# The first layer's output product in one written order with alternating accumulators, and the last projection's partial sums loaded behind the next weights

## The chip, the cores and the metric

The kernel runs as one program on one core of a Trainium2 chip. Engines of that core work side by side, each through its own list of instructions in order: TensorE (PE, matrix products), VectorE (DVE), ScalarE (ACT), GpSimd (POOL) and SyncE (SP, which issues most transfers). An instruction waits on semaphores for what it needs. The metric is the device time of one execution in microseconds (us). The kernel before takes 1270.09 us, the median of three runs (1269.7 to 1270.78).

## What is computed

A stream x of 1024 tokens with 1024 channels goes through two layers; all data is fp32.

```python
# layer 0 (even): a convolution branch A and a recurrent branch B
va, vg, ga, xb, gb = split(h @ w_in)
y_a = conformer_conv(va, vg) * silu(ga)
y_b = rglru_branch(xb, h0 from the context) * silu(gb)
x = x + gate0 * (concatenate([y_a, y_b]) @ w_out)
# layer 1 (odd): pooling mixer
u, g = split(rmsnorm_and_modulate(x) @ w_in1)
y = grouped(pool(u) - u) * scale * silu(g)          # 2048 channels
x = x + gate1 * (y @ w_out1)
return rmsnorm(x, final_g)
```

## The kernel before

Channels lie on partitions and tokens along the free dimension, so x is eight tiles of 128x1024. A large product is computed as three products of rounded halves: `split` makes a high half by a cast on ACT (L98) and a low half by a subtraction on DVE (L99), and `prod` issues high by high (L1153), high by low data (L1155) and low by high (L1156), four times in turn, which makes twelve matmuls of 128x512.

The products of this case are done in two-by-two blocks with seven products in place of eight (a scheme like Strassen's). One call of `quad` makes two tiles of output channels, m and m+1, over both halves of the tokens. The seven operands of data are called b11, t1, t2, b21, t3, b22 and t4; the seven operands of weights, `wq_..._1` to `_7`, are made by `wquad_steps` from two raw loads of 512 KB (`wr_..._0` and `_1`, L1117) by sums on DVE (L1133 to L1142) and splits. There are two raw buffers, so the loads of the next block wait until the last reader of this block's raw weights has run. The products go into three accumulators of one PSUM bank each, a, b and c (tiles `qa`, `qb`, `qc`): b11 into a, which ACT copies to b; t1 into c; t2 on top of the copy in b; b21 on top of a; t3 on top of b; b22 on top of c; t4 on top of b. Between the products the content is read out: c after t1 goes to quarter (1,1), b after t2 to (0,1), a after b21 to (0,0), b after t3 to (1,1), c after b22 to (0,1), and b after t4 to (1,0). A product that adds to a bank has to wait until the reader of the bank's earlier content is done.

The first layer's output product of branch A is `woa`, four calls for m = 0, 2, 4, 6. Its `put` (L1470 to L1482) reads a partial stream back into an x tile, adds the gated accumulator with one DVE instruction (L1473), stores the tile, and adds its square to the sums of the next norm (L1459, L1462, L1463). After it on PE come folds of the second layer's weights, then eight blocks of that layer's products.

The second layer's output product comes in two parts over the input channels, `wo0` (m = 0 to 6) and `wo1`. `wo0` uses another function, `quad_linked`. There each product is made to follow the one before in the written order (`linked`), every second block takes other banks (`spare`: tiles `qac` and half of a wide tile), and the last product of a block (t4) is issued after the next block's b11 and t1 (`pend`). Its `put` loads a 256 KB piece xp of the stream kept in DRAM (L1908), adds the gated accumulator (`gated`, L1829) and stores the piece back from ACT's queue (`stores`, L1845).

The order of instructions on each engine is set when the kernel is built: a scheduler puts each instruction where its own model of time has it ready, `tc.high_priority` lets the read-outs of accumulators go ahead, and `tc.issue_after` keeps one instruction behind another. On the chip the order is fixed. In `woa` before, the order of the seven products on PE comes from that scheduler.

Of the kernel before, what the change touches and what calls it, by code (L numbers as in the profile page):

```python
# [20 lines left out]
KT = D // P  # L21
H = 512
HALF = (slice(0, H), slice(H, S))
# [28 lines left out]
def body(ctx, tc, xT, ctxT, cc, ccol, modT, modW, win, gw, wout, wu, grp, wg, wo1, small, edge, ident, outT):  # L52
# [1412 lines left out]
    def woa(m, w, ahead):  # L1465
# [17 lines left out]
        return quad(w, f"woa{m}", ya, put, ahead, m == KT - 2)  # L1483
# [45 lines left out]
    last["pe"] = ended_[0]  # L1529
# [310 lines left out]
    copied_, kept_out = [None], []  # L1840

    def stores(after, n):
        with held(after):
            for _ in range(n):
                nc.scalar.dma_start(*kept_out.pop(0))  # L1845

    chain = [None]

    def linked(*args):
        with held(chain[0]):  # L1850
            chain[0] = prod(*args)
        return chain[0]

    def spare(name):
        a, c = banks(f"qac_{name}", 0)
        return a, c, wide(f"qb_{name}")[:, HALF[1]]

    def quad_linked(w, name, ops, put, ahead, order, pend, other):
        p1, p2, p3, p4, p5, p6, p7 = w
        a, c, b = spare(name) if other else [psum(f"q{n}_{name}") for n in "acb"]  # L1860
        linked(a, p1, ops["b11"], True, False)
        with tc.high_priority(offset=EVAC):
            evac = nc.scalar.copy(b, a)
        linked(c, p5, ops["t1"], True, False)
        with tc.high_priority(offset=EVAC):
            put(1, 1, c, 0)
            stores(kept_[0], len(kept_out))
        if pend is not None:
            pend()
        linked(b, p6, ops["t2"], False, False)  # L1870
        with tc.high_priority(offset=EVAC):
            put(0, 1, b, 0)
        linked(a, p2, ops["b21"], False, True)
        with tc.high_priority(offset=EVAC):
            put(0, 0, a, None)
        with tc.issue_after(evac.ins):
            nxt_ = ahead()
        for name in order:
            if name == "t3":
                linked(b, p7, ops["t3"], False, False)  # L1880
                with tc.high_priority(offset=EVAC):
                    put(1, 1, b, 1)
            else:
                linked(c, p3, ops["b22"], False, True)
                with tc.high_priority(offset=EVAC):
                    put(0, 1, c, 1)
# [423 lines left out]
```

## Time and profile before

| quantity | value |
|---|---|
| median of three runs | 1270.09 us |
| the profiled execution's own time | 1268.66 us |
| its span from first to last instruction | 1266.9 us |
| PE busy | 1251.0 us, 99% |
| DVE busy | 1140.9 us, 90% |
| ACT busy | 655.1 us, 52% |
| POOL busy | 295.0 us, 23% |
| mean clock granted to TensorE | 0.996 |

Times in rows of the timeline are microseconds from the start of the span. A row gives the start, the busy time, the engine, the line, the operation, the output and inputs, how many were merged, and in brackets the idle time before it and who ended that. Issues of transfers stand under the queue of their engine (SPq, ACTq).

### The profile page before, as it was taken

To read this page: it belongs to the slowest core of one execution; us is meant where nothing else is said; L and a number is where in the kernel's file an instruction comes from. 1 tells how busy PE (TensorE), PEld (TensorE's weight loads), DVE (VectorE), ACT (ScalarE), POOL (GpSimd) and SP (SyncE) were. 2 spreads that over 40 slices of the span, in tenths; PEclk is the share of its full clock that TensorE was granted. 3 is DMA by queue.
4 is the path that set the end of the run, shared out by engine and by line. 5 is a ranking of instruction groups with operands and counts; after the bars stand their busy time and mean duration, and the time that the engine had idled before them with its cause. 6 is when DMAs were issued, how large, how long until landed. Compare 5 with 4: busy or idle time off the path is not lost. (4 is left out here: it accounts for less than half of the span.)

```text
span 1266.9 us, 16191 instructions
## 1 busy us (share of the span) xinstructions
PE 1251.0 (99%) x5858; PEld 1034.7 (82%) x5858; DVE 1140.9 (90%) x1748; ACT 655.1 (52%) x955; POOL 295.0 (23%) x176
## 2 busy tenths in 40 slices
PE   9999999999999999999999999999999999999996
PEld 7788888888888888888887888788888888877885
DVE  7799999999999999988978979999899987977976
ACT  8464566556666533237435446744343444634642
POOL 0015364436443547533210023000000000000003
PEclk9999999999999999999999999999999999999998
DMA  9971121112121234442437665243333334848723
GB/s 377 381 257 33 53 64 50 59 42 75 44 81 42 83 125 133 158 141 84 160 98 233 207 205 173 100 158 125 133 107 118 117 125 142 296 168 311 295 68 133
DMA packets 78705, 182.29 MB, mean 144 GB/s; under 512 B 7712, under 2 KB 23328, under 8 KB 78624
## 3 DMA queue, kind: packets, MB, share of 16 engines
q1 hardware_dynamic: 67328, 172.33, 39.8%
q10 hardware_dynamic: 11296, 8.92, 2.2%
q8 instruction: 46, 0.75, 0.2%
q14 instruction: 35, 0.29, 0.1%
HBM read 137.18 MB, written 44.04 MB: 143 GB/s over the span
## 5 line engine op out<-in xcount | busy, mean ns | idle before, releaser
L670 DVE SCALAR_TENSOR_TENSOR conv<-u,sm,conv 128x505 f32<-128x505 f32 (+6 forms) x224 | 153.8, 746 | 1.0
L2030 POOL TENSOR_TENSOR o<-x,rr 128x256 f32<-128x256 f32 (+1 forms) x10 | 9.7, 1008 | 449.5 <-ACT rr L2030 449.5
L670 ACT ACTIVATE l<-g,sm 128x512 f32<-128x512 f32 (+1 forms) x96 | 58.7, 619 | 57.7 <-PE g L670 57.0
L670 POOL TENSOR_TENSOR l<-l,l 128x1280 f32<-128x1280 f32 x16 | 47.1, 2966 | 25.6 <-ACT l L670 15.1
L98 ACT CAST wq_g<-wr_g 128x512 fp32r<-128x512 f32 x48 | 28.3, 621 | 43.4 <-DMA wr_g<-wg 16.1
L98 ACT CAST wq_wo<-wr_wo 128x512 fp32r<-128x512 f32 x48 | 28.6, 619 | 41.9 <-DMA wr_wo<-wo 20.9
L670 PE MATMUL va<-h0h,wl_va 128*128 128x512 f32 x128 | 49.9, 390 | 0.2 <-DVE wl_va L670 0.2
L670 PE MATMUL gb<-h0h,wl_gb 128*128 128x512 f32 x128 | 49.9, 390 | 0.2 <-POOL wl_gb L670 0.2
L670 PE MATMUL gb<-h0l,wh_gb 128*128 128x512 f32 x128 | 49.8, 389 | 0.0
L670 PE MATMUL gb<-h0h,wh_gb 128*128 128x512 f32 x128 | 49.8, 389 | 0.0
L670 PE MATMUL va<-h0l,wh_va 128*128 128x512 f32 x128 | 49.8, 389 | 0.0
L670 PE MATMUL va<-h0h,wh_va 128*128 128x512 f32 x128 | 49.8, 389 | 0.0
L670 PE MATMUL wob<-ybh,wh_wob 128*128 128x512 f32 x128 | 49.8, 389 | 0.0
L670 PE MATMUL wob<-ybl,wh_wob 128*128 128x512 f32 x128 | 49.8, 389 | 0.0
L670 PE MATMUL wob<-ybh,wl_wob 128*128 128x512 f32 x128 | 49.8, 389 | 0.0
L670 DVE TENSOR_TENSOR_SCAN l<-l,l 128x256 f32<-128x256 f32 (+1 forms) x32 | 48.7, 1521 | 1.1
L670 DVE SCALAR_TENSOR_TENSOR conv<-cL,wsum,conv 128x506 f32<-128x506 f32 (+3 forms) x70 | 48.2, 746 | 0.2
L670 POOL TENSOR_TENSOR l<-l,uc 128x1280 f32<-128x1280 f32 x16 | 47.7, 3008 | 0.0
L98 ACT CAST wq_v<-wr_v 128x512 fp32r<-128x512 f32 x48 | 28.2, 620 | 34.4 <-DMA wr_v<-wfold 15.9
L99 DVE TENSOR_TENSOR wq_wo<-wr_wo,wq_wo 128x512 fp32r<-128x512 f32 x48 | 32.0, 686 | 13.7 <-ACT wq_wo L98 13.6
L670 PE MATMUL xb<-h0l,wh_xb 128*128 128x512 f32 x112 | 43.8, 391 | 0.0
L670 PE MATMUL xb<-h0h,wh_xb 128*128 128x512 f32 x112 | 43.8, 391 | 0.0
(656 smaller groups left out, 4350.3 us busy)
## 6 DMA issues: line engine op xcount, KB each, us to landing
modw<-modW SPq DMA_DIRECT2D x16, 512.0 KB, 10.2
mod<-modT SPq DMA_DIRECT2D x32, 256.0 KB, 3.4
wr_v<-wfold SPq DMA_DIRECT2D x16, 512.0 KB, 4.1
wr_g<-wg SPq DMA_DIRECT2D x16, 512.0 KB, 4.4
wr_wo<-wo SPq DMA_DIRECT2D x16, 512.0 KB, 5.1
mod<-modT SPq DMA_DIRECT2D x14, 512.0 KB, 4.5
y_b<-y SPq DMA_DIRECT2D x24, 256.0 KB, 3.7
y_t<-y SPq DMA_DIRECT2D x24, 256.0 KB, 3.4
```

The source lines that it names most:

```text
L98: return (nc.scalar.copy(hi, src), eng.tensor_tensor(out=lo, in0=src, in1=hi.bitcast(F32), op=sub))
L99: eng.tensor_tensor(out=lo, in0=src, in1=hi.bitcast(F32), op=sub))
L670: last[eng] = f(*args, **kw)
L2030: tail[eng] = f(*args, **kw)
```

## The change

`quad_linked` and its helpers move up in the file so that `woa` can use them too. `woa` now issues its products in a written order: b11, t1, the t4 of the block before, t2, b21, and then t3 and b22 for m = 0 or b22 and t3 for the others. Blocks 2 and 6 use the spare banks. The last t4 is issued after the loop. In `quad_linked` the next block's weights (`ahead`) are now written ahead of the read-out of a. In `wo0` the load of xp is held behind the latest weight load written before it, `loaded[0]`, and that is the next block's for every piece from (0,0) on.

```diff
+    def quad_linked(w, name, ops, put, ahead, order, pend, other):
+        p1, p2, p3, p4, p5, p6, p7 = w
+        a, c, b = spare(name) if other else [psum(f"q{n}_{name}") for n in "acb"]
+        linked(a, p1, ops["b11"], True, False)
+        with tc.high_priority(offset=EVAC):
+            evac = nc.scalar.copy(b, a)
+        linked(c, p5, ops["t1"], True, False)
+        with tc.high_priority(offset=EVAC):
+            put(1, 1, c, 0)
+            if kept_out:
+                stores(kept_[0], len(kept_out))
+        if pend is not None:
+            pend()
+        linked(b, p6, ops["t2"], False, False)
+        with tc.high_priority(offset=EVAC):
+            put(0, 1, b, 0)
+        linked(a, p2, ops["b21"], False, True)
+        with tc.issue_after(evac.ins):
+            nxt_ = ahead()
+        with tc.high_priority(offset=EVAC):
+            put(0, 0, a, None)
+        for name in order:
+            if name == "t3":
+                linked(b, p7, ops["t3"], False, False)
+                with tc.high_priority(offset=EVAC):
+                    put(1, 1, b, 1)
+            else:
+                linked(c, p3, ops["b22"], False, True)
+                with tc.high_priority(offset=EVAC):
+                    put(0, 1, c, 1)
+
+        def last():
+            linked(b, p4, ops["t4"], False, True)
+            with tc.high_priority(offset=EVAC):
+                put(1, 0, b, None)
+        return nxt_, last
...
-        return quad(w, f"woa{m}", ya, put, ahead, m == KT - 2)
+        return quad_linked(w, f"woa{m}", ya, put, ahead, ("b22", "t3") if m else ("t3", "b22"), pend, m % 4 == 2)
...
+    last_ = None
     for m in range(0, KT, 2):
-        w0 = woa(m, w0, lambda: woa_ahead(m))
+        w0, last_ = woa(m, w0, lambda: woa_ahead(m), last_)
+    last_()
...
             t = (vtile, lambda name: atile(name)[:, :H])[xp_n[0] % 2](f"xp{m}_{i}_{h}")
-            nc.sync.dma_start(t, x1_part[m + i][:, HALF[h]])
+            with tc.issue_after(loaded[0].ins):
+                nc.sync.dma_start(t, x1_part[m + i][:, HALF[h]])
```

In the rows of the order that follow, a name such as `wq_woa2_5` is operand 5 of the weights of `woa`'s block m = 2, a final h or l stands for the high or low half, and the last number is a buffer's.

PE in the first block of `woa`, at the end of b21, before:

```order
L1153 MATMUL qa_woa0_5687<-ya_b21h1_5132,wq_woa0_2_5634 128x512
L1155 MATMUL qa_woa0_5687<-ya_b21l1_5134,wq_woa0_2_5634 128x512
L1156 MATMUL qa_woa0_5687<-ya_b21h1_5132,wq_woa0_2_5634 128x512
L1153 MATMUL qa_woa2_5829<-ya_b11h0_5119,wq_woa2_1_5751 128x512
L1155 MATMUL qa_woa2_5829<-ya_b11l0_5121,wq_woa2_1_5751 128x512
L1153 MATMUL qc_woa0_5688<-ya_b22h0_5659,wq_woa0_3_5641 128x512
L1155 MATMUL qc_woa0_5688<-ya_b22l0_5661,wq_woa0_3_5641 128x512
```

and now:

```order
L1153 MATMUL qa_woa0_5687<-ya_b21h1_5132,wq_woa0_2_5634 128x512
L1155 MATMUL qa_woa0_5687<-ya_b21l1_5134,wq_woa0_2_5634 128x512
L1156 MATMUL qa_woa0_5687<-ya_b21h1_5132,wq_woa0_2_5634 128x512
L1153 MATMUL qb_woa0_5689<-ya_t3h0_5647,wq_woa0_7_5637 128x512
L1155 MATMUL qb_woa0_5689<-ya_t3l0_5649,wq_woa0_7_5637 128x512
```

Before, two matmuls of the next block and then b22 follow b21; now t3 follows, which adds to the bank `qb_woa0`.

DVE at the same place, where `qb_woa0` is read into `x1_0` (the third argument of that read is the gate), before:

```order
L1473 SCALAR_TENSOR_TENSOR x1_1_5686<-qc_woa0_5688,m0_132,x1_1_5686 128x512
L99 TENSOR_TENSOR ya_t4l0_5673<-u4_2402,ya_t4h0_5671 128x512
L99 TENSOR_TENSOR ya_t4l0_5673<-u5_2735,ya_t4h0_5671 128x512
L99 TENSOR_TENSOR ya_t4l1_5674<-u6_3069,ya_t4h1_5672 128x512
L99 TENSOR_TENSOR ya_t4l1_5674<-u7_3402,ya_t4h1_5672 128x512
L1473 SCALAR_TENSOR_TENSOR x1_0_5685<-qb_woa0_5689,m0_132,x1_0_5685 128x512
L99 TENSOR_TENSOR wq_woa2_1_5751<-wr_woa2_0_5747,wq_woa2_1_5751 128x512
```

and now:

```order
L1528 SCALAR_TENSOR_TENSOR x1_1_5686<-qc_woa0_5688,m0_132,x1_1_5686 128x512
L99 TENSOR_TENSOR ya_t4l0_5673<-u4_2402,ya_t4h0_5671 128x512
L99 TENSOR_TENSOR ya_t4l0_5673<-u5_2735,ya_t4h0_5671 128x512
L99 TENSOR_TENSOR ya_t4l1_5674<-u6_3069,ya_t4h1_5672 128x512
L1528 SCALAR_TENSOR_TENSOR x1_0_5685<-qb_woa0_5689,m0_132,x1_0_5685 128x512
L99 TENSOR_TENSOR ya_t4l1_5674<-u7_3402,ya_t4h1_5672 128x512
L99 TENSOR_TENSOR wq_woa2_1_5747<-wr_woa2_0_5743,wq_woa2_1_5747 128x512
```

The read of `qb_woa0` moved ahead of one of the four splits of t4; three still stand before it.

PE at the end of `woa`, from the last matmuls of the product ahead of t4 to t4 of block 6, before:

```order
L1153 MATMUL qc_woa6_6179<-ya_b22h1_5660,wq_woa6_3_6097 128x512
L1155 MATMUL qc_woa6_6179<-ya_b22l1_5662,wq_woa6_3_6097 128x512
L1156 MATMUL qc_woa6_6179<-ya_b22h1_5660,wq_woa6_3_6097 128x512
L1153 MATMUL qb_woa6_6180<-ya_t4h0_5671,wq_woa6_4_6100 128x512
L1155 MATMUL qb_woa6_6180<-ya_t4l0_5673,wq_woa6_4_6100 128x512
```

and now:

```order
L1153 MATMUL qb_woa6_6163<-ya_t3h1_5648,wq_woa6_7_6087 128x512
L1155 MATMUL qb_woa6_6163<-ya_t3l1_5650,wq_woa6_7_6087 128x512
L1156 MATMUL qb_woa6_6163<-ya_t3h1_5648,wq_woa6_7_6087 128x512
L1153 MATMUL qb_woa6_6163<-ya_t4h0_5671,wq_woa6_4_6094 128x512
L1155 MATMUL qb_woa6_6163<-ya_t4l0_5673,wq_woa6_4_6094 128x512
```

Before, b22 in bank c stood between t3 and t4 of bank b; now t3 is followed by t4 in the same bank.

DVE in `wo0`, where the weights of block 2 are made and block 0 is read out (a tile `s1_` or a bank `qc_` with itself among the inputs is the sum of two read-outs, L1915 before and L1919 now), before:

```order
L1829 SCALAR_TENSOR_TENSOR xp0_0_0_9414<-qa_wo0_0_9358,m1_134,xp0_0_0_9414 128x512
L99 TENSOR_TENSOR y0_b22l1_9342<-yr_0_b22_1_9339,y0_b22h1_9341 128x1024
L99 TENSOR_TENSOR wq_wo0_2_1_9425<-wr_wo0_2_0_9421,wq_wo0_2_1_9425 128x512
L1133 TENSOR_TENSOR ws_wo0_2_9428<-wr_wo0_2_0_9421,wr_wo0_2_1_9423 128x512
L1915 TENSOR_TENSOR s1_wo0_0_9386<-b_wo0_0_9469,s1_wo0_0_9386 128x512
L1134 TENSOR_TENSOR wr_wo0_2_1_9423<-wr_wo0_2_1_9423 128x512
L1829 SCALAR_TENSOR_TENSOR xp0_1_1_9467<-s1_wo0_0_9386,m1_134,xp0_1_1_9467 128x512
L1135 TENSOR_TENSOR wr_wo0_2_0_9421<-wr_wo0_2_1_9423,wr_wo0_2_0_9421 128x512
L1915 TENSOR_TENSOR qc_wo0_0_9359<-qc_wo0_0_9359,s0_wo0_0_9400 128x512
L99 TENSOR_TENSOR wq_wo0_2_5_9432<-wr_wo0_2_1_9423,wq_wo0_2_5_9432 128x512
```

and now:

```order
L99 TENSOR_TENSOR y0_b22l1_9342<-yr_0_b22_1_9339,y0_b22h1_9341 128x1024
L99 TENSOR_TENSOR wq_wo0_2_1_9422<-wr_wo0_2_0_9418,wq_wo0_2_1_9422 128x512
L1133 TENSOR_TENSOR ws_wo0_2_9425<-wr_wo0_2_0_9418,wr_wo0_2_1_9420 128x512
L1886 SCALAR_TENSOR_TENSOR xp0_0_0_9452<-qa_wo0_0_9358,m1_134,xp0_0_0_9452 128x512
L1919 TENSOR_TENSOR s1_wo0_0_9386<-b_wo0_0_9469,s1_wo0_0_9386 128x512
L1134 TENSOR_TENSOR wr_wo0_2_1_9420<-wr_wo0_2_1_9420 128x512
L1886 SCALAR_TENSOR_TENSOR xp0_1_1_9467<-s1_wo0_0_9386,m1_134,xp0_1_1_9467 128x512
L1919 TENSOR_TENSOR qc_wo0_0_9359<-qc_wo0_0_9359,s0_wo0_0_9400 128x512
L1135 TENSOR_TENSOR wr_wo0_2_0_9418<-wr_wo0_2_1_9420,wr_wo0_2_0_9418 128x512
L99 TENSOR_TENSOR wq_wo0_2_7_9442<-ws_wo0_2_9425,wq_wo0_2_7_9442 128x512
L99 TENSOR_TENSOR wq_wo0_2_5_9429<-wr_wo0_2_1_9420,wq_wo0_2_5_9429 128x512
```

The read-out `xp0_0_0` went from ahead of the weights of block 2 to between `ws_wo0_2` and the sums behind it, and `wq_wo0_2_7` now stands ahead of `wq_wo0_2_5`.

SP at the weights of block 6, before:

```order
L1908 DMA xp2_1_0_9697<-x1_part3_110 128x512
L1681 DMA y_t2_1_102<-y14_9128 128x512
L1908 DMA xp4_0_1_9771<-x1_part4_111 128x512
L1681 DMA y_t4_1_106<-y15_9129 128x512
L1117 DMA wr_wo0_6_0_9729<-wo1 128x1024
L1908 DMA xp4_1_1_9787<-x1_part5_112 128x512
L1117 DMA wr_wo0_6_1_9731<-wo1 128x1024
L1704 DMA yr_1_t1_0_9795<-y_t1_1_101 128x1024
```

and now:

```order
L1912 DMA xp2_1_0_9697<-x1_part3_110 128x512
L1738 DMA y_t2_1_102<-y14_9128 128x512
L1738 DMA y_t4_1_106<-y15_9129 128x512
L1117 DMA wr_wo0_6_0_9726<-wo1 128x1024
L1117 DMA wr_wo0_6_1_9728<-wo1 128x1024
L1912 DMA xp4_0_0_9756<-x1_part4_111 128x512
L1912 DMA xp4_0_1_9771<-x1_part4_111 128x512
L1912 DMA xp4_1_1_9787<-x1_part5_112 128x512
```

The two weight loads stand together now, and two pieces xp of block 4 that were issued ahead of them, and one between them, follow them. At the weights of block 2 the four pieces xp of block 0 likewise follow the weights; before, all four were issued many transfers ahead of them.

More of the change, by code (lines that the diff above doesn't have):

```diff
@@ L1463, in square_acc, with stores, linked, spare @@
             added[0] = nc.vector.tensor_tensor(out=acc_, in0=acc_, in1=q, op=add)
-    def woa(m, w, ahead):
+    copied_, kept_out = [None], []
+    def stores(after, n):
+        with held(after):
+            for _ in range(n):
+                nc.scalar.dma_start(*kept_out.pop(0))
+    linked_ = [None]
+    def linked(*args):
+        with held(linked_[0]):
+            linked_[0] = prod(*args)
+        return linked_[0]
+    def spare(name):
+        a, c = banks(f"qac_{name}", 0)
+        return a, c, wide(f"qb_{name}")[:, HALF[1]]
+    def quad_linked(w, name, ops, put, ahead, order, pend, other):
[33 more added lines that the diff above has]
+        return nxt_, last
+    def woa(m, w, ahead, pend):
         for q in range(2):
@@ L1838, in copied @@
         return t
[L1840 to L1886, printed above, removed]
-        def last():
-            linked(b, p4, ops["t4"], False, True)
-            with tc.high_priority(offset=EVAC):
-                put(1, 0, b, None)
-        return nxt_, last
     def second_late():
```

4 lines of the change are left out of this document (2 added, 2 removed).

## The prediction

> **What bounds the kernel now.** I read the page's busy times first.
>
> ```profile
> span 1266.9 us, 16191 instructions
> PE 1251.0 (99%) x5858; PEld 1034.7 (82%) x5858; DVE 1140.9 (90%) x1748; ACT 655.1 (52%) x955; POOL 295.0 (23%) x176
> ```
>
> PE is busy 99% of its span, so the time moves only by what PE waits, and a stage matters by its PE gaps. The windows of the stages at which the change works, and one between them, say where they are (PE is the second figure, the granted clock follows POOL).
>
> ```profile
> 666.00:706.00 40.00, 39.39 (x171) 31.56 (x169) 34.34 (x60) 19.87 (x36) 0.00 (x0) 1.00 0.70 221
> 706.00:744.50 38.50, 38.22 (x168) 31.65 (x169) 35.51 (x79) 16.36 (x24) 1.32 (x5) 1.00 0.68 224
> 800.00:1090.00 290.00, 290.00 (x1281) 239.89 (x1280) 262.60 (x460) 128.50 (x225) 0.24 (x2) 1.00 0.38 129
> 1090.00:1120.00 30.00, 29.23 (x130) 23.82 (x129) 27.64 (x38) 21.09 (x32) 0.00 (x0) 1.00 0.63 220
> 1120.00:1160.00 40.00, 39.23 (x172) 31.89 (x171) 29.38 (x46) 16.82 (x28) 0.00 (x0) 1.00 0.72 256
> ```
>
> `woa` runs from 666 to 744.5 and PE lacks some 0.9 us in it; the second layer's products from 800 to 1090 lack nothing, so a delay that reaches them is carried on unchanged and nothing there makes it up; `wo0` lacks about 1.5 us from 1090 to 1160. Then the waits of PE in `woa` and, behind the dots, in `wo0` with the start of `wo1`.
>
> ```profile
> PE qb_woa L1153 <- ACT qb_woa L1172: 0.7, 1, 0.7
> PE qc_woa L1153 <- DVE x L1473: 0.2, 1, 0.2
> ...
> PE qac_wo L1156 <- DVE wq_wo L99: 1.2, 2, 0.8
> PE qc_wo L1155 <- DVE y_b22l L99: 0.4, 1, 0.4
> PE qac_wo L1153 <- ACT wq_wo L98: 0.3, 1, 0.3
> ```
>
> These are all the waits that the change could remove. DVE and ACT appear as releasers, so the order on DVE beside PE decides.
>
> **Part 1, `woa`.** The timeline gives the start of the stage, the two places in its first block, and the first fold behind it.
>
> ```profile
> 666.48 0.39 PE L1153 MATMUL qa_woa<-ya_b11h,wq_woa 128*128 128x512 f32 x1
> ...
> 677.36 0.39 PE L1153 MATMUL qa_woa<-ya_b11h,wq_woa 128*128 128x512 f32 x1
> ...
> 678.20 0.50 PE L1153 MATMUL qc_woa<-ya_b22h,wq_woa 128*128 128x512 f32 x1 [0.23 <-DVE x L1473]
> ...
> 744.50 0.39 PE L670 MATMUL fold<-gh,wh_wu 128*128 128x512 f32 x1
> ```
>
> From 666.48 to 677.36 are four products in 10.88 us, 2.72 each. The 28 products take 76.16 us and the stage took 78.02 (744.50 less 666.48), so 1.86 us of delay are in it. The bracketed idle is less than that because rows overlap: a matmul is shown with 0.39 and the next starts 0.227 (2.72 over 12) after it, which hides 0.16, and the first matmul behind a wait shows 0.50, 0.11 more. A wait thus costs its idle time and about 0.28.
>
> The written order lets t3 follow b21 at 677.36 in block 0. It adds to bank b and has to wait until DVE has read t2's result from it. DVE then has no idle time:
>
> ```profile
> 677.40 0.75 DVE L1473 SCALAR_TENSOR_TENSOR x<-qc_woa,m,x 128x512 f32<-128x512 f32 x1
> 678.06 2.48 DVE L99 TENSOR_TENSOR ya_t4l<-u,ya_t4h 128x512 fp32r<-128x512 f32 x4
> 680.47 0.74 DVE L1473 SCALAR_TENSOR_TENSOR x<-qb_woa,m,x 128x512 f32<-128x512 f32 x1
> ```
>
> The read of qc at 677.40 stays where it is; the scheduler of the new order puts three splits of t4, 0.60 us each (2.41 us for four from 678.06 to 680.47), between it and the read of qb. That read starts at 678.06 + 1.81 = 679.87 and ends at 680.62. PE started at 678.20, 0.05 behind the end of qc's read (677.40 + 0.75), so t3 starts at 680.67, 3.31 us late. With the 24 remaining products (65.28) and 0.11 for the first matmul PE is at 746.06. The old delays are not in this sum: the copy that b waits for has t1 and the postponed t4 behind it now, 5.4 us of cover, and the b22 that waited for qc comes later.
>
> At the end of block 6 the new order has t3 and then t4, both in b, with no product between.
>
> ```profile
> 738.84 0.39 PE L1156 MATMUL qb_woa<-ya_t3h,wq_woa 128*128 128x512 f32 x1
> ...
> 739.26 0.75 DVE L1473 SCALAR_TENSOR_TENSOR x<-qb_woa,m,x 128x512 f32<-128x512 f32 x1 [0.31 <-PE qb_woa L1156]
> ```
>
> The last matmul of t3 started at 738.84 and DVE's read of it at 739.26; with 0.75 for the read and 0.05 after it PE could go on at 740.06, where it would want 738.84 + 0.227 = 739.07. That is 1.0 us, and 0.11 more behind the wait; before, b22 covered it. The stage ends at 747.2, against 744.50: **+2.7 us**. The low end is -0.8, if only the last wait is there (76.16 + 1.1 against 78.02); the high end is +4.2, if the delays other than the one at 678.20 (1.86 less 0.39) stay as well. I take 2.7 since every instruction in the sum has its row. The folds follow at once, and what DVE and ACT do for the norm hangs on the same last read, so I let the delay through whole.
>
> **Part 2, block 2 of `wo0`.** Rows of the window, the issue of the weights, and what follows on ACT, DVE and PE:
>
> ```profile
> 1104.00:1108.00 4.00, 4.00 (x19) 3.34 (x18) 3.81 (x6) 3.54 (x4) 0.00 (x0) 1.00 1.00 373
> ...
> 1104.12 0.94 SPq L1117 DMA_DIRECT2D wr_wo<-wo  x2
> ...
> 1110.55 0.62 ACT L98 CAST wq_wo<-wr_wo 128x512 fp32r<-128x512 f32 x1 [2.76 <-DMA wr_wo<-wo]
> ...
> 1106.89 0.74 DVE L1829 SCALAR_TENSOR_TENSOR xp<-qa_wo,m,xp 128x512 f32<-128x512 f32 x1
> ...
> 1111.81 0.69 DVE L1133 TENSOR_TENSOR ws_wo<-wr_wo,wr_wo 128x512 f32<-128x512 f32 x1
> ...
> 1113.01 0.69 DVE L1134 TENSOR_TENSOR wr_wo<-wr_wo 128x512 f32<-128x512 f32 x1
> ...
> 1115.48 0.68 DVE L99 TENSOR_TENSOR wq_wo<-wr_wo,wq_wo 128x512 fp32r<-128x512 f32 x1
> ...
> 1116.22 0.50 PE L1156 MATMUL qac_wo<-y_t1h,wq_wo 128*128 128x512 f32 x1 [0.77 <-DVE wq_wo L99]
> ```
>
> PE waits for the low half of operand 5, made at 1115.48; it costs 0.77 + 0.28 = 1.05 us. Before, the pieces xp of block 0 had come long before, and the read-out at 1106.89 ran while DVE had room. Now they are issued behind these weights. The first weight had landed when ACT's wait of 2.76 us ended at 1110.55; the second was read at 1111.81. A piece of 0.262 MB takes 0.70 us at the 373 GB/s of the window, so xp0_0_0 is there at about 1112.5, just after `ws` (1111.81 + 0.60). In the new order DVE runs from there: xp0_0_0 1112.5, sum 1113.16, L1134 1113.76 (1113.01 before), xp0_1_1 1114.36, sum 1115.02, L1135 1115.62, operand 7 at 1116.22, operand 5 at 1116.82, with 0.66 behind a read-out and 0.60 behind the others. That is 1.34 later than 1115.48: **+1.3 us**, on the chain that PE waits for. The store of xp0_0_0 waits in ACT's queue ahead of the casts of operands 7 and 5, but at 1113.25 it is done before L1134 lets the cast go. Low end: -1.05, if the transfers taken out ahead of the weights let them land that much earlier. High end: +3.0, if a piece is waited for as long as one is at 1145.61 in the rows below (1.71 us). I take the chain: in the order before, eleven other transfers stand between the last pieces' old place and the weights, and the window shows the engines full with those.
>
> **Part 2, block 6.** Issues on SP, a read-out, ACT's wait for the weights, and PE's two waits:
>
> ```profile
> 1141.56 0.69 SPq L1681 DMA_DIRECT2D y_t<-y  x1
> 1143.14 0.32 SPq L1908 DMA_DIRECT2D xp<-x_part  x1
> ...
> 1143.99 0.42 SPq L1117 DMA_DIRECT2D wr_wo<-wo  x1
> ...
> 1145.41 0.33 SPq L1117 DMA_DIRECT2D wr_wo<-wo  x1
> ...
> 1145.61 0.75 DVE L1829 SCALAR_TENSOR_TENSOR xp<-qb_wo,m,xp 128x512 f32<-128x512 f32 x1 [1.71 <-DMA xp<-x_part]
> ...
> 1149.95 1.14 ACT L98 CAST wq_wo<-wr_wo 128x512 fp32r<-128x512 f32 x2 [6.00 <-DMA wr_wo<-wo]
> ...
> 1154.43 0.50 PE L1153 MATMUL qac_wo<-y_t1h,wq_wo 128*128 128x512 f32 x1 [0.29 <-ACT wq_wo L98]
> ...
> 1155.64 0.50 PE L1156 MATMUL qac_wo<-y_t1h,wq_wo 128*128 128x512 f32 x1 [0.48 <-DVE wq_wo L99]
> ```
>
> Two pieces xp of block 4 stood ahead of the weights (one at 1143.14) and one between them. Without them the last y store can follow the issues that end at 1142.25 (1141.56 + 0.69), the first weight comes at about 1142.7, 1.3 us earlier, and the second, whose buffer DVE frees in this stretch, at about 1143.3, 2.1 us earlier. ACT idled 6.00 us until the first, so the making of operand 5 starts 1.3 us earlier, but one more read-out (0.66) now stands ahead of its low half. PE's two waits cost 0.29 + 0.48 + 0.56 = 1.33 us: the high half takes back the first, 0.57, the low half some 0.2 of the second. I take **-0.8 us**; the ends are -1.33 (they cannot give more) and +0.7 (only the extra read-out). Block 4's weights are issued when DVE frees their buffers, and the xp of block 2 were issued before that without delaying them, so I cost them 0 (ends -0.3 and +0.7, one read-out). `wo1`'s start may gain from the earlier DVE, 0.4 + 0.28 at most; its weights are also freed by DVE, so 0. The new place of the first stores and of `ahead` costs no instruction.
>
> **Sum.** 2.7 + 1.3 - 0.8 = +3.2 us on the profiled 1268.66 us (span 1266.9), thus 1271.9; the median lies 1.43 higher, thus 1270.09 + 3.2 = **1273.3 us**. About 0.2%, 2.5 us, is what a measurement of this kernel can tell from no change.
>
> **A rule on the clock.** The wait of 3.3 us would be PE's longest. At the end of the kernel PE's work is sparse and the clock falls:
>
> ```profile
> 1256.27 0.68 PE L2030 MATMUL fin_ms<-dg,ones 128*128 128x256 f32 x2
> 1257.56 1.08 PE L2030 MATMUL fin_ms<-dg,ones 128*128 128x256 f32 x2 [0.62 <-DVE dg L2030]
> ...
> 1258.00:1259.00 1.00, 0.65 (x2) 0.00 (x0) 1.00 (x4) 0.32 (x1) 1.00 (x3) 0.50 0.86 326
> ```
>
> Two matmuls of 128x256 show 0.68 us, and 1.08 as the clock goes to 0.50, although no gap there is over 0.62. Waits up to 0.77 in `wo0` left it at 1.00. The Trainium skill, "TensorE: Matmul & The Clock Gate", section on the HAM clock gate, says that the clock halves after an idle window of about 3.4 us that runs freely, and returns after a busy one. By it this wait would just not fill a window; if it did, an estimate from its window is 1.7 us more.
>
> **The rivals.**
> - *The clock falls in the wait of `woa`.* If half clock lasts as long as the wait, 3.3 us, half of that is lost: +1.65, 1274.9. For it: the fall at the end. Against: all other windows at 1.00. It decides from the length of the idle.
> - *The pieces are free.* The weights of block 2 land earlier for the transfers gone from ahead of them and DVE has slack: 0 instead of 1.3, block 6 and `wo1` give 1.33 and 0.7: 2.7 - 2.0 = +0.7, 1270.8, no change. For it: DMA was full at 1104 to 1108. Against: DVE's order.
> - *The other side: DVE reaches qb in time.* If DVE is 3.3 us ahead at 677.40 t3 waits for nothing, `woa` gives -0.8 (written order and spare banks), block 6 and `wo1` -1.33 and -0.7, block 2 0: -2.8, 1267.3. It decides whether the read ends before 677.36. Against: no idle in DVE's rows here and the same rows ahead of it.
> - *Reads of xp block the weights in each block:* block 2 at +3.0, block 6 at +0.7: 2.7 + 3.7 = +6.4, 1276.5. For it: the 1.71 us wait at 1145.61. Against: a piece adds only 0.7 behind a weight.
>
> **How the numbers follow.** Forecast 0.50 (own range 1271.7 to 1274.7), clock 0.08, pieces free 0.20, other side 0.12, blocked 0.10. Slower by over 0.2%, above 1272.6: clock, blocked and 0.33 of the forecast, 0.51; within: 0.17 of the forecast, pieces free and 0.01 of the other side, 0.38; faster 0.11. The range 1269.4 to 1276.2 leaves out the other side and most of blocked.
>
> **What would show it.** A row of PE with over 3 us idle near 680, released by DVE's read L1528, and one near 746 of about 0.8; the first fold near 747.2. In `wo0`, the t1 of block 2 waiting about 2.1 us idle for operand 5, and that of block 6 hardly. If no wait over 1 us stands in the first block of `woa`, the forecast is wrong.

## The result and the profile after

The changed kernel takes 1273.79 us, the median of ten runs (1272.08 to 1275.61), against 1270.14 us for the kernel before (ten runs, 1268.69 to 1272.39). The ratio is 1.0029, with a 95% interval of 1.002 to 1.0037: slower by 3.65 us, where 3.2 had been forecast. The profiled execution took 1272.08 us.

The busy times of the kernel after, from its page:

```profile
span 1270.3 us, 16192 instructions
PE 1251.1 (98%) x5858; PEld 1036.0 (82%) x5858; DVE 1141.3 (90%) x1748; ACT 655.5 (52%) x955; POOL 293.6 (23%) x176
```

Its windows of the same stages as before (PE is the second figure, the granted clock follows POOL):

```profile
666.00:706.00 40.00, 36.86 (x157) 30.14 (x156) 33.31 (x58) 18.70 (x33) 0.00 (x0) 0.96 0.66 217
706.00:749.45 43.45, 42.61 (x189) 34.93 (x188) 37.03 (x79) 17.67 (x26) 1.32 (x5) 1.00 0.60 196
800.00:1090.00 290.00, 289.75 (x1278) 239.50 (x1277) 264.26 (x464) 130.10 (x230) 0.70 (x6) 1.00 0.38 129
1090.00:1120.00 30.00, 29.69 (x131) 24.24 (x130) 26.93 (x36) 22.48 (x33) 0.00 (x0) 1.00 0.76 259
1120.00:1160.00 40.00, 39.56 (x174) 32.78 (x175) 30.31 (x46) 15.90 (x28) 0.00 (x0) 1.00 0.71 249
```

PE's busy time is nearly the same, 1251.1 us against 1251.0, and the span is 3.4 us longer, so PE stands idle longer. The windows show where: in the first it is busy 36.86 us of 40 where it was 39.39, and its clock is 0.96 where it was 1.00. `wo0`, in the last two windows, lacks 0.75 us where it lacked 1.54. PE's waits in `woa`, and behind the dots in `wo0` and the start of `wo1`:

```profile
PE qb_woa L1153 <- DVE x L1528: 4.0, 2, 3.1
...
PE qc_wo L1155 <- DVE y_b22l L99: 0.8, 1, 0.8
PE qac_wo L1156 <- DVE wq_wo L99: 0.8, 1, 0.8
```

Both waits in `woa` are for bank b, and no old one is left. The timeline on PE shows the start of the stage, the two waits with the end of t3 between them, and the first fold; then DVE's rows at the first wait.

```profile
667.31 0.39 PE L1153 MATMUL qa_woa<-ya_b11h,wq_woa 128*128 128x512 f32 x1
...
677.97 0.39 PE L1156 MATMUL qa_woa<-ya_b21h,wq_woa 128*128 128x512 f32 x1
681.50 0.80 PE L1153 MATMUL qb_woa<-ya_t3h,wq_woa 128*128 128x512 f32 x1 [3.14 <-DVE x L1528]
682.09 0.63 PE L1155 MATMUL qb_woa<-ya_t3l,wq_woa 128*128 128x512 f32 x1
...
685.73 0.39 PE L1153 MATMUL qc_woa<-ya_b22h,wq_woa 128*128 128x512 f32 x1
...
746.57 0.50 PE L1153 MATMUL qb_woa<-ya_t4h,wq_woa 128*128 128x512 f32 x1 [0.84 <-DVE x L1528]
...
749.45 0.39 PE L670 MATMUL fold<-gh,wh_wu 128*128 128x512 f32 x1
...
678.23 0.75 DVE L1528 SCALAR_TENSOR_TENSOR x<-qc_woa,m,x 128x512 f32<-128x512 f32 x1
678.89 1.89 DVE L99 TENSOR_TENSOR ya_t4l<-u,ya_t4h 128x512 fp32r<-128x512 f32 x3
680.70 0.75 DVE L1528 SCALAR_TENSOR_TENSOR x<-qb_woa,m,x 128x512 f32<-128x512 f32 x1
```

The read of qb starts at 680.70, behind three splits, and PE goes on at 681.50, which is 0.75 for the read and 0.05 after it. PE would have gone on at 677.97 + 0.227 = 678.20, so the wait costs 3.30 us. What the forecast did not have is in the next rows: the matmuls of t3 show 0.63 in place of 0.39, and t3 takes 685.73 - 681.50 = 4.23 us in place of 2.72, 1.51 more. Of that, 0.11 is what the first matmul behind a wait costs anyway; the rest is the clock, which fell to half at 681.06, still during the wait:

```profile
677.65:681.06 3.41, 0.70 (x4) 0.24 (x2) 3.41 (x7) 1.14 (x2) 0.00 (x0) 1.00 0.91 299
681.06:684.47 3.41, 2.97 (x7) 2.42 (x8) 3.41 (x7) 0.53 (x1) 0.00 (x0) 0.50 0.97 305
```

The two profiled executions differ by 3.42 us. By PE's rows it comes from these places (differences of unrounded times; the rounded rows give 78.02 and 82.14 for `woa`):

| place | before, us | after, us | difference |
|---|---|---|---|
| start of the span to the start of `woa` | 666.48 | 667.31 | +0.83 |
| `woa` to the first fold | 78.03 | 82.13 | +4.11 |
| first fold to the start of `wo0` | 348.54 | 347.87 | -0.67 |
| `wo0` and `wo1` | 125.35 | 124.39 | -0.96 |
| rest | | | +0.11 |

The first row lies ahead of the change; another execution of the same kernel (below) reaches `woa` at 665.96, so that difference belongs to the execution. The stretch between fold and `wo0` is code that the change leaves alone; it took between 347.87 and 349.83 us in the fourteen profiles of this case, so nothing is read into the -0.67.

In `wo0`, the rows at block 2 of the kernel after: the cast of the first weight on ACT, the sums and read-outs on DVE, then t1 on PE.

```profile
1113.47 0.62 ACT L98 CAST wq_wo<-wr_wo 128x512 fp32r<-128x512 f32 x1 [1.65 <-DMA wr_wo<-wo]
...
1114.73 0.68 DVE L1133 TENSOR_TENSOR ws_wo<-wr_wo,wr_wo 128x512 f32<-128x512 f32 x1
1115.36 0.75 DVE L1886 SCALAR_TENSOR_TENSOR xp<-qa_wo,m,xp 128x512 f32<-128x512 f32 x1
...
1119.69 0.69 DVE L99 TENSOR_TENSOR wq_wo<-wr_wo,wq_wo 128x512 fp32r<-128x512 f32 x1
...
1119.07 0.39 PE L1153 MATMUL qac_wo<-y_t1h,wq_wo 128*128 128x512 f32 x1
...
1120.44 0.50 PE L1156 MATMUL qac_wo<-y_t1h,wq_wo 128*128 128x512 f32 x1 [0.75 <-DVE wq_wo L99]
```

The one row of the kernel before that the comparison needs is the first matmul of t1:

```profile
1114.84 0.39 PE L1153 MATMUL qac_wo<-y_t1h,wq_wo 128*128 128x512 f32 x1
```

DVE needs 1119.69 - 1114.73 = 4.96 us from the first sum to operand 5, where it needed 1115.48 - 1111.81 = 3.67: the chain is 1.29 longer, as forecast. But the cast of the first weight comes 1119.07 - 1113.47 = 5.60 us ahead of t1, where it came 1114.84 - 1110.55 = 4.29 ahead. The weights are there 1.31 us earlier by PE's own progress, and PE waits 0.75 us where it waited 0.77. At block 6 PE waits for nothing; the two weights are issued together and ACT idles 3.05 us for them where it idled 6.00:

```profile
1146.39 1.66 SPq L1117 DMA_DIRECT2D wr_wo<-wo  x2
...
1151.23 1.14 ACT L98 CAST wq_wo<-wr_wo 128x512 fp32r<-128x512 f32 x2 [3.05 <-DMA wr_wo<-wo]
...
1168.43 0.75 DVE L1886 SCALAR_TENSOR_TENSOR xp<-qb_wo,m,xp 128x512 f32<-128x512 f32 x1 [2.36 <-DMA xp<-x_part]
...
1196.17 0.50 PE L1155 MATMUL qc_wo<-y_b22l,wq_wo 128*128 128x512 f32 x1 [0.84 <-DVE y_b22l L99]
```

The last two rows are a loss that the forecast put at 0: DVE now idles 2.36 us for a piece of block 4, and the wait in `wo1` is 0.84 where it was 0.4. That the first leads to the second is argued, not shown.

### The profile page after: what moved, and what is told of

Same layout as the page of the kernel before. It is cut to its first block, busy times and chain, and to the rows that moved or that the text cites. A ratio compares the mean times of both kernels' runs of the same rounds, so it can differ in the third digit from the quotient of the medians.

```text
span 1270.3 us, 16192 instructions
## 1 busy us (share of the span) xinstructions
PE 1251.1 (98%) x5858; PEld 1036.0 (82%) x5858; DVE 1141.3 (90%) x1748; ACT 655.5 (52%) x955; POOL 293.6 (23%) x176
## 4 chain that ended last, share of the span: by engine, by line
PE 68%; DVE 20%; DMA 7%; issue 2%; ACT 2%; POOL 1%; POOLq 0%; SPq 0%; ACTq 0%; DVEq 0%
DVE conv L670 6%; PE wob L670 6%; PE va L670 5%; PE xb L670 4%; PE vg L670 4%; DVE l L670 3%; PE fold L670 3%; PE g L670 3%; PE ga L670 2%; PE ga L161 2%; PE ga L162 2%; PE ga L163 2%; PE qb_v L1153 2%; DMA wr_wo<-wo 2%; PE qb_v L1155 2%
## 5 line engine op out<-in xcount | busy, mean ns | idle before, releaser
L670 PE MATMUL xb<-h0h,wl_xb 128*128 128x512 f32 x112 | 43.6, 389 | 0.0
```

What stands on the lines that cost most here:

```text
L670: last[eng] = f(*args, **kw)
```

## The experiments

The theory to be tested was: part 1 costs 2.7 us, by the order of DVE's instructions ahead of t3 and by the last t4, and more when the clock falls; part 2 is close to nothing. All edits are relative to the kernel after. Each ratio is to executions of the kernel before that were timed beside it; there are three such sets of runs. "`woa`" below is the time from its first matmul to the first fold, 78.03 us before and 82.13 after.

**Each part alone.** Part 1 alone leaves the loads of xp where they were, and the next block's weights in `wo0` too:

```diff
-        with tc.issue_after(evac.ins):
-            nxt_ = ahead()
+        early = name.startswith("woa")
+        if early:
+            with tc.issue_after(evac.ins):
+                nxt_ = ahead()
         with tc.high_priority(offset=EVAC):
             put(0, 0, a, None)
+        if not early:
+            with tc.issue_after(evac.ins):
+                nxt_ = ahead()
...
-            with tc.issue_after(loaded[0].ins):
-                nc.sync.dma_start(t, x1_part[m + i][:, HALF[h]])
+            nc.sync.dma_start(t, x1_part[m + i][:, HALF[h]])
```

> Part 1 alone: woa in the written order, wo0 as before. Theory (the cost lies in woa: two waits of t3 and t4, and a stretch at half clock behind the first): the stage takes 4.1 us longer than before's 78.0, PE idles about 3.1 us ahead of t3 of block 0 and the granted clock falls to 0.50 behind it; 1274.2 us against 1270.1. The waits in wo0 are those of before (block 2 about 1.05, block 6 about 1.33). Rival (the second part carries part of the cost, the first costs only its waits of 2.7): 1272.8 and no fall of the clock without the second part.

Measured: 1274.35 us (five runs), ratio 1.0036 [1.0023, 1.005]. The median lies 4.1 us above that of the kernel before; the ratio gives +4.6, between +2.9 and +6.4. Its profiled execution was the quickest of the five, 1270.94 us. In its rows the wait is the same, but the clock holds:

```profile
681.08 0.50 PE L1153 MATMUL qb_woa<-ya_t3h,wq_woa 128*128 128x512 f32 x1 [3.14 <-DVE x L1533]
681.42 0.40 PE L1155 MATMUL qb_woa<-ya_t3l,wq_woa 128*128 128x512 f32 x1
```

The windows behind the wait show the granted clock at 1.00:

```profile
681.00:683.00 2.00, 1.92 (x8) 1.61 (x9) 2.00 (x5) 0.00 (x0) 0.00 (x0) 1.00 0.95 329
683.00:685.00 2.00, 2.00 (x10) 1.66 (x9) 2.00 (x4) 0.63 (x1) 0.00 (x0) 1.00 0.92 224
```

`woa` took 80.75 us, 2.72 more than before. That is the +2.7 of the prediction without the fall, seen in an execution that had none.

Part 2 alone calls the old function for `woa`:

```diff
-        return quad_linked(w, f"woa{m}", ya, put, ahead, ("b22", "t3") if m else ("t3", "b22"), pend, m % 4 == 2)
+        return quad(w, f"woa{m}", ya, put, ahead, m == KT - 2)
...
-    last_ = None
     for m in range(0, KT, 2):
-        w0, last_ = woa(m, w0, lambda: woa_ahead(m), last_)
-    last_()
+        w0 = woa(m, w0, lambda: woa_ahead(m))
```

> Part 2 alone: woa by the scheduler's order, wo0 with xp behind the next weights. Theory (block 2 loses nothing because its weights land as much earlier as the chain on DVE got longer; block 6 gains its 1.33; wo1's first block loses 0.4): 1269.1 us, 1.0 below before; t1 of block 2 waits 0.75, that of block 6 nothing. Rival (the prediction's sum for this part, +1.3 - 0.8): 1270.6, with about 2.1 us idle at block 2.

Measured: 1269.34 us, ratio 0.9993 [0.9984, 1.0001]: between 2.0 us faster and no change. `woa` took 78.03 us as before, and `wo0` with `wo1` 125.26 against 125.35. So the whole loss lies in part 1, and part 2 is worth nothing that can be told from zero.

**The order in the first block.** Here b22 stands ahead of t3 in block 0 as in the others. The sum of squares over the second half of the tokens then begins with quarter (0,1), which b22 completes, in place of (1,1).

```diff
-                square_acc(nacc[h][:, :H], v, (m, i) == (0, h), f"n1q{m}_{i}_{h}")
-        return quad_linked(w, f"woa{m}", ya, put, ahead, ("b22", "t3") if m else ("t3", "b22"), pend, m % 4 == 2)
+                square_acc(nacc[h][:, :H], v, (m, i) == (0, 0), f"n1q{m}_{i}_{h}")
+        return quad_linked(w, f"woa{m}", ya, put, ahead, ("b22", "t3"), pend, m % 4 == 2)
```

> The changed kernel with b22 ahead of t3 in block 0 of woa too (the sums of squares then begin with quarter (0,1)). Theory: b22 waits for the read of qc, about 0.9 us, and t3 finds b free; the 3.3 us wait becomes 0.9 and the clock stays at 1.00, so 2.4 + 1.4 = 3.8 us less than the changed kernel, 1270.0 against 1273.8. Rival (DVE, not the order on PE, sets the pace there and a later product pays what this one saves): within 1 us of the changed kernel. Rival (the slow matmuls are not the idle's doing): 2.4 less, 1271.4, and t3 is still slow.

Measured: 1270.22 us, ratio 1.0001 [0.9991, 1.0011], against 1.0029 and 1.0032 for the kernel after in its two timings. PE's waits in `woa`:

```profile
PE qb_woa L1153 <- DVE x L1528: 0.8, 1, 0.8
PE qc_woa L1153 <- ACT wq_woa L98: 0.8, 1, 0.8
```

`woa` took 78.43 us. The wait of 3.1 us is gone, and the clock holds. What comes in its place is a wait of 0.8 us of b22 for its weights. The order of two products in one block carries 3.7 us of `woa` (82.13 less 78.43).

**The order at the end.** In block 6, t3 now stands ahead of b22, so that b22 lies between t3 and t4 of bank b; block 0 is left as in the kernel after.

```diff
-        return quad_linked(w, f"woa{m}", ya, put, ahead, ("b22", "t3") if m else ("t3", "b22"), pend, m % 4 == 2)
+        return quad_linked(w, f"woa{m}", ya, put, ahead, ("b22", "t3") if m in (2, 4) else ("t3", "b22"), pend, m % 4 == 2)
```

> The changed kernel with t3 ahead of b22 in block 6 of woa too, so that b22 stands between t3 and the last t4. Theory: the wait ahead of the last t4, 0.84 us idle and 1.1 in all, is gone: 1272.7 against 1273.8. Rival (DVE reads late there anyway and the fold or b22 pays it): within 0.3 of 1273.8. The 3.1 us idle of block 0 is as in the changed kernel, so this profile is one more throw on whether the clock falls behind it: if it falls each time, t3 takes 4.2 us, if it depends on the moment, 2.85 or 4.2.

Measured: 1273.06 us, ratio 1.0021 [1.0012, 1.003]. The wait of the last t4 is gone, in its place t3 of block 6 starts 0.31 late and takes 0.17 longer, and `woa` takes 81.44, 0.69 less than after. The clock falls here too (t3 of block 0 takes 1.50 us too long).

**Both orders.** Block 0 with b22 first and block 6 with t3 first:

```diff
-                square_acc(nacc[h][:, :H], v, (m, i) == (0, h), f"n1q{m}_{i}_{h}")
-        return quad_linked(w, f"woa{m}", ya, put, ahead, ("b22", "t3") if m else ("t3", "b22"), pend, m % 4 == 2)
+                square_acc(nacc[h][:, :H], v, (m, i) == (0, 0), f"n1q{m}_{i}_{h}")
+        return quad_linked(w, f"woa{m}", ya, put, ahead, ("b22", "t3") if m < KT - 2 else ("t3", "b22"), pend, m % 4 == 2)
```

> The changed kernel with b22 ahead of t3 in block 0 and t3 ahead of b22 in block 6 (and the sums of squares begun with quarter (0,1)). Theory: both new waits go, woa takes 77.3 us against 78.0 before, and with what the second part gives the time is 1269.0, under both kernels. Rival (woa gains no more than it did with b22 first, 78.4, or wo0 pays): 1270.2.

Measured: 1270.54 us, ratio 1.0012 [1.0002, 1.0023]. `woa` took 78.29 us, hardly less than with the first order alone (78.43): with t3 straight behind b21 in block 6, the wait for the read of bank b, 0.8 us, has moved from t4 to t3. The expected 77.3 was missed, and the rival holds.

**Work in the wait.** Twelve matmuls that nobody reads are put between b21 and t3 of block 0. The result is untouched; the kernel does one product more.

```diff
+        if name == "woa0":
+            f = banks("fill", 0)[0]
+            linked(f, p1, ops["b11"], True, False)
         for name in order:
```

> The changed kernel with one product more: between b21 and t3 of block 0 the twelve matmuls of b11 are done once more into a bank that nobody reads. The wait of t3 ends when it did, but PE idles 0.6 us and not 3.1. Theory (the idle drops the clock): t3 takes 2.8 us and not 4.2, granted clock 1.00 throughout, 1.4 us less than the changed kernel, 1272.4 against 1273.8. Rival (t3 is slow for another cause, its operands or DVE beside it): t3 takes 4.2 us again, 1273.8. Rival (the filler delays t3): 1274 or more.

Measured: 1274.29 us, ratio 1.0032 [1.0021, 1.0043]. In the window at the place of the wait PE is busy and the clock holds, and `woa` takes 80.73 us, 1.40 less than after. The window:

```profile
681.00:683.00 2.00, 1.58 (x8) 1.25 (x8) 2.00 (x4) 0.62 (x1) 0.00 (x0) 1.00 0.80 242
```

The time shows nothing of it: the ratio is that of the kernel after. In the timeline on PE stands a wait in the second layer's products that the kernel after doesn't have:

```profile
825.64 0.50 PE L1153 MATMUL qa_v<-x_b11h,wq_v 128*128 128x512 f32 x1 [1.56 <-ACT wq_v L98]
```

> The kernel with the filling product once more, beside the changed kernel in the same call. Theory (the idle drops the clock in most executions, 1.4 us each): about 1.1 less than the changed kernel; the wait of 1.56 us at 825 that stood in the first profile is of that execution and is not there again. Rival (the filler only moves the loss, to the first products of the second layer): that wait is there again and the time is that of the changed kernel.

A second timing of the same kernel: 1272.6 us (six runs), ratio 1.0026 [1.0011, 1.004]. `woa` took 80.83 us, the clock held again, and the wait at 825 is there again:

```profile
825.62 0.50 PE L1153 MATMUL qa_v<-x_b11h,wq_v 128*128 128x512 f32 x1 [1.27 <-ACT wq_v L98]
```

It is the cast of a weight whose load comes late: issued 71.8 to 71.9 us behind the first fold, as in the kernel after, the load takes 5.0 us (4.7 in the second profile) to land in place of 3.2. Why it does so in the two profiles with the added product and in no other is not settled. Beside this second timing the kernel after took 1274.16 us (below), and the intervals of the two ratios overlap. So the price of the fall is shown within `woa` and not in the total.

**How often the clock falls.** The kernel after was run again: one single execution, and eight timed ones.

> The changed kernel once more, for its profile alone. If the 3.1 us idle of PE in block 0 of woa always drops the clock, t3 shows 4.2 us and a granted clock of 0.50 again; if it depends on where the idle falls, it may show 2.85 us and a clock of 1.00.

> The changed kernel beside the one with the filling product, 1273.8 by the runs so far; a third profile of it, with the clock down to 0.50 behind the 3.1 us idle or not.

Measured: 1272.43 us for the single execution; 1274.16 us, ratio 1.0032 [1.0021, 1.0042], for the timed ones. The clock fell in both profiles. In the single execution it fell only when PE was at work again; these are t3's first matmul and the place in it where the matmuls grow longer:

```profile
680.14 0.50 PE L1153 MATMUL qb_woa<-ya_t3h,wq_woa 128*128 128x512 f32 x1 [3.14 <-DVE x L1528]
...
681.40 0.39 PE L1156 MATMUL qb_woa<-ya_t3h,wq_woa 128*128 128x512 f32 x1
681.63 0.58 PE L1153 MATMUL qb_woa<-ya_t3h,wq_woa 128*128 128x512 f32 x1
682.01 0.63 PE L1155 MATMUL qb_woa<-ya_t3l,wq_woa 128*128 128x512 f32 x1
```

With part 1 alone, the swapped end and the kernel of the next paragraph, six profiles have the idle of 3.14 or 3.15 us. The clock fell in five, where t3 and b22 took 1.50 to 1.76 us longer than two products do, and held in one, where they took 0.13 longer; the fall thus costs 1.4 to 1.6 us.

Why the same idle brings the fall or not can be read from the granted clock in the traces. In all fourteen profiles every stretch at full clock lasts a whole multiple of 3.413 us from its rise to its fall (675.839 us, 198 times, ahead of the fall in the kernel after), and each of the five falls near 681 lasts 3.413 us. So in these traces the clock changes only on a grid of 3.413 us, and the grid lies differently against the program in each execution. Cut along it, the windows around the wait are these, first in the single execution of the kernel after, then behind the dots in part 1 alone:

```profile
674.85:678.26 3.41, 2.15 (x10) 1.45 (x8) 3.41 (x7) 2.52 (x5) 0.00 (x0) 1.00 0.90 299
678.26:681.67 3.41, 1.53 (x7) 1.27 (x8) 3.41 (x6) 0.00 (x0) 0.00 (x0) 1.00 0.94 327
681.67:685.08 3.41, 3.41 (x10) 2.64 (x9) 3.38 (x7) 1.25 (x2) 0.00 (x0) 0.50 0.88 243
...
676.07:679.48 3.41, 1.87 (x9) 1.22 (x7) 3.41 (x7) 2.24 (x5) 0.00 (x0) 1.00 0.94 283
679.48:682.89 3.41, 1.81 (x8) 1.51 (x9) 3.41 (x7) 0.00 (x0) 0.00 (x0) 1.00 0.93 313
```

In the first, the window from 678.26 held 1.88 us of the idle, PE was busy 1.53 us in it, and the clock halved at its end. In the second, the grid cut the idle into two parts of 1.54 and 1.60 us; PE was busy 1.87 and 1.81 us in the two windows, and the clock held. In the other four profiles PE was busy 0.63 to 0.74 us in the window ahead of the fall. Of all such windows of the fourteen profiles up to the last products, those with 1.70 us busy or more kept the clock, those with 1.53 or less lost it, and none lies between. At the kernel's end, with matmuls of 128x256 and narrower, the clock fell behind windows with 2.38 to 2.90 us busy by the rows, so the figure is one for the dense 128x512 stream alone. An estimate from it: an idle of 3.14 us that falls at random on the grid leaves less than 1.71 to 1.88 us in each window, and so the clock up, in 8 to 18% of the executions.

The granted clock, averaged over the whole of each timed execution (recorded to three places), says the same for the executions without a profile:

| kernels | mean granted clock (executions) |
|---|---|
| before, in the three sets | 0.9958 (25), 0.9960 (27), 0.9962 (25) |
| with the idle of 3.1 us: after twice, part 1 alone, end swapped, block 0 early | 0.9943 (10), 0.9945 (8), 0.9944 (5), 0.9946 (11), 0.9950 (9) |
| without it: part 2 alone, b22 first, both orders, reads ahead of the splits (below) twice | 0.9964 (11), 0.9961 (11), 0.9959 (12), 0.9960 (11), 0.9960 (11) |
| filled: twice | 0.9961 (9), 0.9963 (6) |

A fall takes half of 3.41 us, 1.71 us of clock, which is 0.0013 of 1270 us. The second group lies some 0.0015 below the others: most of its executions had the fall, and filling the wait prevents it. Of its 43 executions the 20 with a mean clock of 0.993 or 0.994 took 1274.3 us in the mean and the 8 with 0.996 or 0.997 took 1271.4. That agrees with a price in the total, but doesn't show it for this fall alone: in the filled kernel, too, the executions with less clock are the longer ones (1276.0 us for four at 0.995, 1272.6 for seven at 0.997).

**Block 0's pieces early.** Only the four pieces of block 0 go back to their old place, ahead of block 2's weights:

```diff
-            with tc.issue_after(loaded[0].ins):
+            with tc.issue_after(loaded[0].ins) if m else nullcontext():
                 nc.sync.dma_start(t, x1_part[m + i][:, HALF[h]])
```

> The changed kernel, but the four pieces xp of block 0 of wo0 are issued as early as before; those of the later blocks stay behind the weights. Theory (the pieces cost the chain on DVE 1.3 us, and their leaving the queue gave the weights of block 2 the same back): the first weight's cast comes about 4.3 us ahead of t1 and not 5.6, the chain is short again, t1 still waits about 0.75 us, the time is that of the changed kernel, 1273.8. Rival (the weights' earlier landing had another cause): the cast stays 5.6 ahead, t1 waits for nothing, 1272.7. Rival (neither matters, other queues decide): t1's wait over 1.3 us.

Measured: 1272.85 us, ratio 1.0026 [1.0017, 1.0036], not to be told from the kernel after (1.0029 and 1.0032). ACT's cast of the first weight, and DVE's making of operand 5's low half (t1 starts at 1119.66 here):

```profile
1114.72 0.62 ACT L98 CAST wq_wo<-wr_wo 128x512 fp32r<-128x512 f32 x1 [1.86 <-DMA wr_wo<-wo]
...
1119.66 0.68 DVE L99 TENSOR_TENSOR wq_wo<-wr_wo,wq_wo 128x512 fp32r<-128x512 f32 x1
```

The cast is 4.94 us ahead of t1, where the kernel after has 5.60. Over all profiles it is 5.16 to 5.93 us ahead in the ten with these pieces behind the weights (mean 5.67), and 4.29 to 4.94 in the four with the pieces early (mean 4.54). The ranges don't meet: with both changes of part 2 the weights come about 1.1 us earlier. Only this kernel moves the pieces alone, and its cast lies 0.73 us behind the mean of the ten; the other three, 4.29 to 4.52, also write the next weights later. So some 0.7 of the 1.1 us are shown for the pieces, by one profile, and the rest is not told apart. PE shows no idle at t1 here, where the theory had 0.75 us. The low half of operand 5 is begun 0.63 us behind the start of t1 in the mean of the ten, 0.40 in the four. So the longer chain on DVE and the earlier weights nearly cancel.

**The reads ahead of the splits.** The splits of b22 and t4 are held behind DVE's read of bank b, so that t3 needn't wait for them; the end is swapped as well.

```diff
-            for i in range(KH):
+            for i in range(KH if name == "t3" else 0):
                 split_op(ya, name, i, kept[name][i])
+    read_ = [None]
+
+    def ya_rest():
+        with tc.issue_after(read_[0].ins):
+            for name in BOPS[5:]:
+                for i in range(KH):
+                    split_op(ya, name, i, kept[name][i])
...
             put(0, 1, b, 0)
+        if name == "woa0":
+            ya_rest()
         linked(a, p2, ops["b21"], False, True)
...
-            nc.vector.scalar_tensor_tensor(out=v, in0=x, scalar=m0[:, 0, 2 * KT + m + i : 2 * KT + m + i + 1],
+            read_[0] = nc.vector.scalar_tensor_tensor(out=v, in0=x, scalar=m0[:, 0, 2 * KT + m + i : 2 * KT + m + i + 1],
                                            in1=v, op0=mult, op1=add)
...
-        return quad_linked(w, f"woa{m}", ya, put, ahead, ("b22", "t3") if m else ("t3", "b22"), pend, m % 4 == 2)
+        return quad_linked(w, f"woa{m}", ya, put, ahead, ("b22", "t3") if m in (2, 4) else ("t3", "b22"), pend, m % 4 == 2)
```

> The changed kernel with the splits of b22 and t4 of woa's first block put behind DVE's read of bank b (before, b22's four and three of t4's stood ahead of it), and with t3 ahead of b22 in block 6. Theory (the new wait is DVE's order: the read of b came seven splits too late): t3 of block 0 waits for nothing, no idle over 1 us in woa, clock 1.00, the stage takes 76.5 to 77.1 us against 78.0 before and 82.1 in the changed kernel; with what the second part gives, 1268.3 us, about 1.7 under before. Rival (DVE as a whole is the limit there, its 20 us without idle only move the wait to b22, t4 or the next block's weights): 78 to 79 us for the stage and 1270.

Measured: 1269.84 us, ratio 1.0001 [0.9992, 1.001]. PE's waits in `woa`:

```profile
PE qac_woa L1156 <- DVE wq_woa L99: 0.5, 1, 0.5
PE qb_woa L1153 <- DVE x L1538: 0.4, 1, 0.4
```

t3 waits for nothing (its delay is 0.09 us), yet `woa` takes 77.96 us, as it did before the change. The waits have gone to block 2's operand 5 and block 4's bank b, both for DVE. The expected 76.5 to 77.1 was missed, and stage and time are the rival's. That the splits held back are in the way later is argued from these releasers, not shown. The same with `wo0` as in the kernel before, thus this diff and the one of part 1 alone together:

> The same as the kernel with the reads first, with wo0 as before (xp not held, weights behind the read-out of a). Theory: woa as there, 76.5 to 77.1; wo0 as before with block 6's 1.3 us of waits, wo1's b22 0.7 instead of 1.2: 1268.9, so 0.6 over the one with both. Rival (the second part gives nothing or costs): the same time or less than the one with both.

Measured: 1271.16 us, ratio 1.0008 [0.9998, 1.0018], and 79.16 us for `woa`, with a wait of 1.7 us at one bank b. No kernel here beats the one before beyond its interval; the nearest is part 2 alone.

## Why the prediction was right, and where its terms were off

- *`woa`, +2.7 us.* Right in mechanism and in both waits: 3.30 and 1.01 us where 3.31 and 1.0 were worked out, released by the read L1528 in both cases. In the execution whose clock held, the stage grew by 2.72. Mis-sized as a whole, since the clock falls in most executions: the stage grew by 4.11 in the profile after.
- *The rival of the clock, +1.65 us with a chance of 0.08.* Its price was right (1.4 to 1.6 measured, with a half clock of 3.41 us where 3.3 was assumed), its chance wrong: five of six. This is the step that failed. The prediction let the length of the idle decide; the same 3.14 us went both ways, and what decided was how long PE was busy in one window of 3.41 us. The argument against the fall was that all windows of the kernel before are at 1.00, but these have no PE wait over 0.77 us and say nothing of one of 3 us; the fall at the end, with gaps of 0.62, was the nearest row and should have weighed more. The Trainium skill, "TensorE: Matmul & The Clock Gate", section on the HAM clock gate, says that the clock halves after an idle window of about 3.4 us that runs freely. Here the clock halved behind a window in which PE was busy 1.53 us of 3.41, so the measurement goes against a whole idle window being needed; that the window runs freely agrees with the grid of 3.413 us, which lies differently in each execution.
- *Block 2 of `wo0`, +1.3 us.* The chain on DVE grew by 1.29 us as worked out, but PE's wait did not grow (0.75 against 0.77). The failed step is the reason given for taking the chain alone, that eleven other transfers stand between the pieces' old place and the weights: the weights land some 1.1 us earlier in the profiles with part 2, some 0.7 of it by taking the pieces out, as far as one profile shows. The low end had that effect, and the rival of the free pieces rested on it; for this block the rival was right.
- *Block 6, -0.8 us.* The direction was right; the waits of 1.33 us are gone altogether, which was the low end. In nine of eleven profiles with the new order these waits cost below 0.6 us; in one, 0.87, and in one, the loads came late and PE lost 3.09.
- *`wo1`, 0.* Off: its first wait grew by about 0.4 us in the pair, and over the profiles the delay there is 1.44 us in the mean of eleven against 0.79 of three.
- *Part 2 as a whole, +0.5 us.* Measured alone -0.9 us, between -2.0 and +0.1; the profiles give 125.1 us for `wo0` and `wo1` in the mean of eleven with it and 124.9 in three without. It is nothing that these runs can tell from zero.
- *The delay is carried through.* The 290 us window of the second layer's products still lacks nothing but 0.25 us, so it made nothing up.
- *The sum, +3.2 us against +3.65.* That it came out so near is luck in part, for two errors have opposite signs: the clock was left out (1.4 to 1.6 us in five of six, about 1.2 in the mean) and part 2 was put 0.5 to 1.4 too high.
- *The other side, DVE in time.* Refuted by the row at 680.70. Where DVE was made to be in time (the reads ahead of the splits), `woa` was no quicker than before: it waits for DVE elsewhere, and the -0.8 of the low end is not to be had by that order.

## What to carry to other kernels

Before an accumulator's order is written by hand, look at what stands on the reading engine between two uses of one bank: here three splits of 0.60 us ahead of one read made PE wait 3.3 us, and swapping two products took that away. A wait's price is its length and, when it is long, the clock: here 3.1 us of idle halved it in five of six profiles, and what decided was where the wait fell on the clock's windows of 3.41 us. So the matmuls behind a wait have to be read in more than one execution. Moving loads behind others is a trade, not a delay alone: what goes ahead lands earlier, and both ends have to be summed.

## What the hardware showed that was not expected

- An idle of 3.14 us halves TensorE's clock in most executions and not in all, and the fall may come when PE is at work again: 1.5 us behind the restart in the second profile of the kernel after (680.14 to 681.63), where it then lasts into the next product (1.29 us lost in t3 and 0.46 in b22). The clock changes only on a grid of 3.413 us; in the dense 128x512 stream it halved for one window of that length behind each window with PE busy 1.53 us or less, and stayed up behind all with 1.70 us or more. Where between the two the limit lies, and what counts as busy for narrower matmuls, was not measured.
- That `woa` was 1.4 us shorter in the filled kernel's rows didn't show in the total in its two timings; in both profiles another wait, of 1.3 to 1.6 us, came 145 us later, and what ties it to the filling is open.
